# Hybrid diffusion step on one core: 28 adaLN pieces from TensorE matmuls to VectorE row sums

## The chip, the core and the metric

The kernel is one program on one NeuronCore of one Trainium2 chip. The metric is the device time of one execution in microseconds (us); lower is better. Three timed runs of the kernel before gave a median of 3042.03 us (3039.22 to 3045.7).

## What is computed

One inference step through two trunk layers (L = 2) for 128 context and 512 latent tokens, T = 640 in all, D = 1024. What matters here of a layer:

```
m = silu(c) @ w_mod[l] + b_mod[l]          # [6 * 1024], for c_ctx (context) and c (latent)
sh1, sc1, g1, sh2, sc2, g2 = split(m, 6)   # parts 0 to 5
h = rmsnorm(x) * (1 + sc1) + sh1
...                                        # four mixers on h, gated and merged
x = x + g1 * merged
h2 = rmsnorm(x) * (1 + sc2) + sh2
x = x + g2 * (square(relu(h2 @ w_fc1)) @ w_fc2)
```

The vector m (adaLN) depends on the conditioning alone, not on x, so it can be made at any time before its use. All data are float32.

## The kernel before

Activations lie transposed, channels on the 128 partitions and tokens along the row. Every large product is done in three matmuls on split operands (a high part and the rest, low): `mm3_step`, lines L225 to L227, 128 x 128 weights against 320 tokens. A *block* is one panel of 128 output channels: 8 k-tiles x 3 matmuls for each half (320 tokens) of T, 48 in all, into one of the two `dn` PSUM banks per half. The weights of a block come as two tiles `wr` on SyncE's DMA queue (L202); ScalarE casts the high part `wh` (L214), and VectorE, or in every third case GpSimd, subtracts the low part `wl` (`sub_lo`, L198). All three rings hold four tiles, two blocks.

The program runs a prologue, then for each layer the mixers (with an order of steps written out in `PLAN`), the output projection (8 blocks), a norm, and the MLP. The MLP goes in four quarters q: 8 blocks of fc1, each half emptied by `squares` (Relu on ScalarE, L1754; product r on VectorE, L1755; cast and `sub_lo` into `fh`, `fl`), then 8 blocks of fc2, each half emptied by `residual` on VectorE (L1547). The order in which instructions stand on each engine is made by a scheduler from the program's order and priorities, and each engine then runs its queue in that order.

adaLN is made in *pieces* of 256 outputs, four to a part, so 24 a layer. `adaln` does a piece on TensorE: 8 small matmuls of `cpad` (the two conditioning vectors, padded to 32 columns) against the weight rows (L290), a copy to SBUF on ScalarE (L295), two matmuls with `sel` that turn the row into columns (L297), and an add of the bias on VectorE (L300) into `mods[l]`. Layer 0's parts 0 and 1 are made in the prologue. The rest go through the generator `adaln_ahead`, which loads four [128, 512] tiles `wa` (256 KB each, ring of 8) per piece and makes one piece per step: 4 during the first mixers, 8 during layer 0's output projection, and then 28 (4 of layer 0's part 5, 24 of layer 1) in layer 0's MLP, where `between`, called after each block, takes five steps of the chain `bgen` in eight blocks. The same chain holds `s5_build` for layer 1 (9 steps): tables for the S5 mixer, complex products `cmul` with one real product on VectorE (L595), its twin on GpSimd (L596) and their sum on VectorE (L597), and small matmuls (L635, L662, L668).

Of the kernel before, what the change touches and what calls it, by code (L numbers as in the profile page):

```python
# [13 lines left out]
F32 = mybir.dt.float32  # L14
# [9 lines left out]
D = 1024  # L24
# [20 lines left out]
RINGS = dict(  # L45
    t1=3, tx=4, tq=6, ty=2, tw=5, td=5, nt=4, wa=8, wr=4, wh=4, wl=4, fh=10,
)
# [28 lines left out]
def hybrid_body(ctx: ExitStack, tc: tile.TileContext, a: dict, o: dict, dbg: dict):  # L76
# [79 lines left out]
    def wa(shape, name):  # L156
        return ring("wa", 512, "ada" if "ada" in top else "pool")(shape, name)

# [148 lines left out]
    def adaln_ahead(l, parts, after=()):  # L307

        for part in parts:
            for q in range(4):  # L310
                halves = {}

                def raw(part, n, q=q, halves=halves):
                    if n not in halves:
                        halves[n] = wa([128, 512], "wa")
                        sp.dma_start(
                            out=halves[n], in_=a["w_mod"][l, part * 4 + q, n // 2][:, (n % 2) * 512:(n % 2) * 512 + 512]
                        )
                    return halves[n]
# [156 lines left out]
    def s5_build(l, where, after):  # L476
# [116 lines left out]
        def cmul(out, xr, yr, xi, yi, op, shape):  # L593
            u, v = big(shape, "s5u", bufs=2, where=where), big(shape, "s5v", bufs=2, where=where)
            nc.vector.tensor_tensor(out=u, in0=xr, in1=yr, op=ALU.mult)  # L595
            nc.gpsimd.tensor_tensor(out=v, in0=xi, in1=yi, op=ALU.mult)  # L596
            nc.vector.tensor_tensor(out=out, in0=u, in1=v, op=op)  # L597
# [945 lines left out]
    def residual(l, part, ps, hf, f, x):  # L1543

        for s, c0, c1 in streams(hf):
            xs = x[:, f, hf * HF + c0:hf * HF + c1]
            nc.vector.scalar_tensor_tensor(  # L1547
                out=xs, in0=ps[:, c0:c1], scalar=mods[l][:, part * 8 + f, s:s + 1], in1=xs, op0=ALU.mult, op1=ALU.add
            )


# [17 lines left out]
    with tc.tile_pool(name="pro", bufs=1, reuse_waits="tile") as pool:  # L1569
# [11 lines left out]
        def panel_adaln(parts, q, acc, out):  # L1581
            w = {part: [big([128, 1024], "wm", bufs=WM) for _ in range(2)] for part in parts}
            for part in parts:
                for i in range(2):
                    sp.dma_start(out=w[part][i], in_=a["w_mod"][0, part * 4 + q, i])
            if soon:
# [37 lines left out]
        build_after[0] = h[1][0:1, KT - 1, T - 1:T].bitcast(F32)  # L1624
        adgen = adaln_ahead(0, range(2, 6), {4: 1})

    for l in range(L):
# [97 lines left out]
        with ExitStack() as mlp:  # L1725
# [3 lines left out]
            acc_n = big([128, T], "acc_n")  # L1729

            def res(part, squares, f, hf, ps):
                residual(l, part, ps, hf, f, x)
                if squares:
                    square_into(acc_n, x, f, hf)

            for f in range(KT - NTAIL):
# [15 lines left out]
            def squares(act, j, hf, ps):  # L1752
                r = t1([128, HF], "r2")
                nc.scalar.activation(out=r, in_=ps, func=AF.Relu)  # L1754
                nc.vector.tensor_tensor(out=r, in0=r, in1=ps, op=ALU.mult)  # L1755
                hi, lo = hsl(act[j], 0, hf)
                nc.scalar.copy(out=hi, in_=r)
                sub_lo(lo, r, hi)

            act0 = []  # L1760
# [24 lines left out]
            def between():  # L1785
                nonlocal turn
                turn += 1
                step(bgen, turn * 5 // 8 - (turn - 1) * 5 // 8)

            for q in range(4):  # L1790
# [4 lines left out]
                for f in range(KT - NTAIL if q == 3 and l + 1 < L else KT):  # L1795
# [42 lines left out]
def _pack(inp):  # L1838
# [3 lines left out]
    for n, s in sizes.items():  # L1842
# [11 lines left out]
    p["x_t"] = np.concatenate([inp["x_prompt"][0], inp["x_sample"][0]], 0).T.reshape(KT, 128, T).transpose(1, 0, 2)  # L1854
    p["c_t"] = np.stack([_col(inp["c_ctx"]), _col(inp["c"][0])], -1)
    p["w_mod"] = st([
        st([
            w.reshape(2, 4, 128, 24, 256)[s, :, :, q].transpose(1, 0, 2).reshape(128, 1024) for q in range(24) for s in range(2)
        ]).reshape(24, 2, 128, 1024) for w in inp["w_mod"]
    ])  # L1860
    p["b_mod"] = _col(inp["b_mod"])
# [126 lines left out]
```

## Time and profile before

| | us |
|---|---|
| median of 3 runs (lowest, highest) | 3042.03 (3039.22, 3045.7) |
| the profiled execution, its own time | 3031.18 |
| span of its profile, first to last instruction | 3029.4 |
| TensorE busy (share of the span) | 2841.5 (94%) |
| VectorE busy | 1724.3 (57%) |
| ScalarE busy | 1180.8 (39%) |
| GpSimd busy | 970.2 (32%) |

The profile is one execution, 10.9 us below the median of the timed runs. Matmuls are pipelined, so a busy TensorE is not one at its peak: how many matmuls it starts in a stretch says more. TensorE's granted clock is full (1.00) in the stretches that are spoken of below but for the one that ends at 1088 us.

### The profile page before, as it was taken

To read this page: it belongs to the slowest core of one execution; us is meant where nothing else is said; L and a number is where in the kernel's file an instruction comes from. 1 tells how busy PE (TensorE), PEld (TensorE's weight loads), DVE (VectorE), ACT (ScalarE), POOL (GpSimd) and SP (SyncE) were. 2 spreads that over 40 slices of the span, in tenths; PEclk is the share of its full clock that TensorE was granted. 3 is DMA by queue.
4 is the path that set the end of the run, shared out by engine and by line. 5 is a ranking of instruction groups with operands and counts; after the bars stand their busy time and mean duration, and the time that the engine had idled before them with its cause. 6 is when DMAs were issued, how large, how long until landed. Compare 5 with 4: busy or idle time off the path is not lost.

```text
span 3029.4 us, 54102 instructions
## 1 busy us (share of the span) xinstructions
PE 2841.5 (94%) x20782; PEld 2663.8 (88%) x20782; DVE 1724.3 (57%) x3730; ACT 1180.8 (39%) x2660; POOL 970.2 (32%) x1057
## 2 busy tenths in 40 slices
PE   7888898999899999999999889999999999999999
PEld 5888788898689888899998879888898999999999
DVE  7859847765643456646235686475666436433333
ACT  4343463343344242323234536523535434322322
POOL 3737506523212222424111670264131122211111
PEclk9989999999899999999999999999999999999999
DMA  6752253224432735434444323431252323222222
GB/s 238 239 180 90 71 152 111 81 90 134 145 109 72 239 102 174 146 115 154 153 146 132 121 82 111 140 107 58 91 181 86 110 87 112 63 77 74 74 77 84
DMA packets 241858, 364.21 MB, mean 120 GB/s; under 512 B 42272, under 2 KB 104480, under 8 KB 241600
## 3 DMA queue, kind: packets, MB, share of 16 engines
q1 hardware_dynamic: 226848, 336.97, 35.5%
q10 hardware_dynamic: 14752, 23.78, 2.1%
q8 instruction: 164, 2.69, 0.4%
q14 instruction: 94, 0.77, 0.1%
HBM read 294.98 MB, written 65.68 MB: 119 GB/s over the span
## 4 chain that ended last, share of the span: by engine, by line
PE 71%; DVE 15%; issue 4%; DMA 3%; ACT 3%; POOL 2%; SPq 0%; ACTq 0%; DVEq 0%; POOLq 0%
PE dn L225 20%; PE dn L226 19%; PE dn L227 19%; DVE wl L198 2%; DVE B L767 2%; PE mx L290 1%; PE mx L1287 1%; PE pb L1331 1%; PE mx L1461 1%; PE mx L1325 1%; PE mx L1416 1%; DMA sseg<-acum 1%; DVE sc L764 1%; DVE sc L765 1%; PE mx L745 1%
## 5 line engine op out<-in xcount | busy, mean ns | idle before, releaser
L198 POOL TENSOR_TENSOR wl<-wr,wh 128x512 fp32r<-128x512 f32 x207 | 282.6, 1366 | 1271.2 <-ACT wh L214 1151.3
L214 ACT CAST wh<-wr 128x512 fp32r<-128x512 f32 (+1 forms) x614 | 377.4, 620 | 612.9 <-PE dn L226 539.6
L198 DVE TENSOR_TENSOR wl<-wr,wh 128x512 fp32r<-128x512 f32 (+1 forms) x407 | 325.7, 804 | 304.7 <-ACT wh L214 297.3
L225 PE MATMUL dn<-hh,wh 128*128 128x320 f32 x1328 | 422.6, 319 | 8.4 <-ACT us L697 2.7
L227 PE MATMUL dn<-hh,wl 128*128 128x320 f32 x1328 | 420.2, 317 | 3.4 <-DVE wl L198 3.4
L226 PE MATMUL dn<-hl,wh 128*128 128x320 f32 x1328 | 420.1, 316 | 2.8 <-DVE hl L403 1.5
L225 PE MATMUL dn<-nh,wh 128*128 128x320 f32 x992 | 311.7, 315 | 6.6 <-DVE r L1755 6.6
L225 PE MATMUL dn<-fh,wh 128*128 128x320 f32 x1008 | 313.6, 311 | 2.0 <-DVE s5u L595 1.3
L226 PE MATMUL dn<-nl,wh 128*128 128x320 f32 x992 | 308.9, 312 | 3.9 <-DVE nl L403 1.6
L227 PE MATMUL dn<-fh,wl 128*128 128x320 f32 x1008 | 312.0, 310 | 0.0
L226 PE MATMUL dn<-fl,wh 128*128 128x320 f32 x1008 | 311.8, 309 | 0.0
L227 PE MATMUL dn<-nh,wl 128*128 128x320 f32 x992 | 308.0, 311 | 0.0
L226 PE MATMUL dn<-wl,hh 128*128 128x256 f32 (+1 forms) x880 | 258.2, 294 | 16.3 <-DVE wl L198 14.2
L225 PEld LDWEIGHTS dn<-hh,wh 128*128 128x128 f32 x1328 | 254.3, 192 | 16.5 <-issue 3.1
L225 PE MATMUL dn<-wh,hh 128*128 128x256 f32 (+1 forms) x880 | 259.7, 297 | 8.5 <-DVE dtraw L1216 4.2
L227 PEld LDWEIGHTS dn<-hh,wl 128*128 128x128 f32 x1328 | 254.2, 191 | 8.9 <-DVE wl L198 4.6
L226 PEld LDWEIGHTS dn<-hl,wh 128*128 128x128 f32 x1328 | 254.2, 191 | 7.1 <-POOL hl L198 2.1
L227 PE MATMUL dn<-wh,hl 128*128 128x256 f32 (+1 forms) x880 | 257.1, 293 | 0.0
L1547 DVE SCALAR_TENSOR_TENSOR x<-dn,mod,x 128x192 f32<-128x192 f32 (+2 forms) x240 | 98.0, 437 | 225.2 <-PE dn L227 222.2
L225 PE MATMUL dn<-B,wh 128*128 128x320 f32 x640 | 207.8, 326 | 15.1 <-ACT B L834 4.4
L226 PE MATMUL dn<-B,wh 128*128 128x320 f32 x640 | 203.4, 318 | 0.0
L227 PE MATMUL dn<-B,wl 128*128 128x320 f32 x640 | 201.3, 315 | 0.0
(400 smaller groups left out, 6715.0 us busy)
## 6 DMA issues: line engine op xcount, KB each, us to landing
wr<-in_w_fc_dram SPq DMA_DIRECT2D x256, 256.0 KB, 2.8
wa<-in_w_mod_dram SPq DMA_DIRECT2D x160, 256.0 KB, 4.5
wr<-in_w_gate_dram SPq DMA_DIRECT2D x128, 256.0 KB, 2.8
wr<-in_w_tok_dram SPq DMA_DIRECT2D x80, 256.0 KB, 2.9
wr<-in_w_branch_dram SPq DMA_DIRECT2D x64, 256.0 KB, 3.0
acc<-gth SPq DMA_DIRECT2D x48, 320.0 KB, 3.0
gold<-acc SPq DMA_DIRECT2D x48, 320.0 KB, 3.3
gate<-gah ACTq DMA_DIRECT2D x70, 160.0 KB, 2.0
```

Source lines behind the costliest of these rows:

```text
L198: engine.tensor_tensor(out=out, in0=full, in1=hi, op=ALU.subtract)
L214: nc.scalar.copy(out=hi, in_=raw)
L225: nc.tensor.matmul(ps, sh, vh, start=first, stop=False)
L226: nc.tensor.matmul(ps, sh, vl, start=False, stop=False)
L227: nc.tensor.matmul(ps, sl, vh, start=False, stop=last)
L290: nc.tensor.matmul(acc[r0:r0 + 32, i * 256:i * 256 + 256], cpad[:, k, :], raw(part, k // 2)[:, c0:c0 + 256], start=(n_ < 4), stop=(n_ >= 4),)
L745: nc.tensor.matmul(xs[:, ri, g * NI:(g + 1) * NI], pm[:, ri, g * 128:(g + 1) * 128], U[:, g0 + g], start=True, stop=True)
L764: ve.tensor_tensor(out=pair[:, 0], in0=src, in1=re.to_broadcast(shp), op=ALU.mult)
L765: ve.tensor_tensor(out=pair[:, 1], in0=src[:, :, ::-1], in1=im.to_broadcast(shp), op=ALU.mult)
L767: ve.tensor_tensor(out=dst, in0=dst, in1=pair[:, i], op=ALU.add)
L1287: nc.tensor.matmul(sc[:, n, c0:c0 + (k1 - k0) * 128], qT[rows[n], g, ct], kT[rows[n], k0:k1].rearrange("p k c -> p (k c)"), start=True, st ...
L1547: nc.vector.scalar_tensor_tensor(out=xs, in0=ps[:, c0:c1], scalar=mods[l][:, part * 8 + f, s:s + 1], in1=xs, op0=ALU.mult, op1=ALU.add)
```

## The change

Layer 0's parts 2 to 4 stay as they were, except that `wa` is now a ring of three [128, 1024] tiles (512 KB). The other 28 pieces become `adaln_rows`: w_mod transposed lies in DRAM, a tile of 128 outputs (rows) by 1024 inputs is loaded, and VectorE multiplies it with the conditioning vector and sums each row in one instruction (`tensor_tensor_reduce`), once for each of the two conditioning vectors, with the bias as the sum's start. The product itself goes to a PSUM tile that nobody reads. That is 56 tiles and 112 row sums. The conditioning vectors, silu applied, are written to DRAM in the prologue and broadcast to all partitions (`cb`, 1 MB) before each MLP. One row sum is taken after each half block, held by the scheduler behind the instruction that empties the half's bank (`fill`); 96 fall into layer 0's MLP and 16 into layer 1's. `between` now steps `s5_build` alone, once in six blocks, and the scratch tiles of its products have one buffer instead of two in the MLP.

```diff
 RINGS = dict(
-    t1=3, tx=4, tq=6, ty=2, tw=5, td=5, nt=4, wa=8, wr=4, wh=4, wl=4, fh=10,
+    t1=3, tx=4, tq=6, ty=2, tw=5, td=5, nt=4, wa=3, wr=4, wh=4, wl=4, fh=10,
 )
...
+    cr = tmp([128, 16], "cr", bufs=1)
+    sp.dma_start(out=cr, in_=a["c_rows"])
+    crt = tmp([128, 16], "crt", bufs=1)
+    nc.scalar.activation(out=crt, in_=cr, func=AF.Tanh, scale=0.5)
+    nc.vector.tensor_scalar(out=crt, in0=crt, scalar1=0.5, scalar2=0.5, op0=ALU.mult, op1=ALU.add)
+    nc.vector.tensor_tensor(out=cr, in0=cr, in1=crt, op=ALU.mult)
+    c_d = dp.tile([128, 16], F32, name="c_d")
+    sp.dma_start(out=c_d, in_=cr)
...
+    def cond_rows():
+
+        cb = big([128, 2, D], "cb")
+        sp.dma_start(out=cb.rearrange("p s k -> p (s k)"), in_=c_d.rearrange("a b -> (a b)").unsqueeze(0).to_broadcast((128, 2 * D)))
+        return cb
+
+    def adaln_rows(l, parts, cb, after=()):
+
+        for part in parts:
+            for f in range(part * 8, part * 8 + 8):
+                with tc.high_priority(offset=AHEAD):
+                    w = wa([128, D], "wa")
+                    sp.dma_start(out=w, in_=a["w_modt"][l * 48 + f - 40])
+                prod = mx().rearrange("p a b -> p (a b)")
+                for s in range(2):
+                    nc.vector.tensor_tensor_reduce(
+                        out=prod, in0=w, in1=cb()[:, s], scale=1.0, scalar=bmod[l][:, f:f + 1], op0=ALU.mult,
+                        op1=ALU.add, accum_out=mods[l][:, f, s:s + 1],
+                    )
+                    if s and f % 8 == 7 and part in after:
+                        make_gsc(l, after[part])
+                    yield
...
         def cmul(out, xr, yr, xi, yi, op, shape):
-            u, v = big(shape, "s5u", bufs=2, where=where), big(shape, "s5v", bufs=2, where=where)
+            u, v = (big(shape, t, bufs=2 if where == "build" else 1, where=where) for t in ("s5u", "s5v"))
...
+            def fill(ins):
+
+                with tc.issue_after(ins.ins):
+                    step(rows)
+
             def res(part, squares, f, hf, ps):
-                residual(l, part, ps, hf, f, x)
+                ins = residual(l, part, ps, hf, f, x)
                 if squares:
                     square_into(acc_n, x, f, hf)
+                fill(ins)
...
             def squares(act, j, hf, ps):
                 r = t1([128, HF], "r2")
                 nc.scalar.activation(out=r, in_=ps, func=AF.Relu)
-                nc.vector.tensor_tensor(out=r, in0=r, in1=ps, op=ALU.mult)
+                ins = nc.vector.tensor_tensor(out=r, in0=r, in1=ps, op=ALU.mult)
                 hi, lo = hsl(act[j], 0, hf)
                 nc.scalar.copy(out=hi, in_=r)
                 sub_lo(lo, r, hi)
+                fill(ins)
...
-            bgen = [adgen]
+            cb = cond_rows()
+            step(adgen, 99)
+            rows, bgen = adaln_rows(l, (5,), lambda: cb), iter(())
             if l + 1 < L:
-                bgen += [
-                    adaln_ahead(l + 1, (0, 1), {1: 0}),
-                    s5_build(l + 1, "mlp", lambda: act0[7][1][0:1, 0, T - 1:T].bitcast(F32)),
-                    adaln_ahead(l + 1, range(2, 6), {4: 1}),
-                ]
-            bgen = itertools.chain(*bgen)
+                rows = itertools.chain(rows, adaln_rows(l + 1, range(5), lambda: cb, {1: 0, 4: 1}))
+                bgen = s5_build(l + 1, "mlp", lambda: act0[7][1][0:1, 0, T - 1:T].bitcast(F32))
...
-                step(bgen, turn * 5 // 8 - (turn - 1) * 5 // 8)
+                step(bgen, int(turn % 6 == 0))
```

What this makes of the instructions' order is shown at three places, as they stand in each engine's queue. Rows of the changed kernel carry its own line numbers: L1795 there is L1755 before, L1578 is L1547, L626 and L628 are L595 and L597, L354 is the new row sum.

The first place is VectorE in the first quarter of layer 0's MLP, where fc1's halves are emptied. Before:

```order
L1755 TENSOR_TENSOR r_2382_12528<-r_2382_12528,dn_12503 128x320
L198 TENSOR_TENSOR fl_12092<-r_2382_12528,fh_12091 128x320
L198 TENSOR_TENSOR wl_12660<-wr_12657,wh_12659 128x512
L198 TENSOR_TENSOR wl_12666<-wr_12663,wh_12665 128x512
L1755 TENSOR_TENSOR r_2384_12558<-r_2384_12558,dn_12533 128x320
L198 TENSOR_TENSOR fl_12092<-r_2384_12558,fh_12091 128x320
L300 TENSOR_TENSOR mod_93<-mx_12571,bmod_89 128x4
L1755 TENSOR_TENSOR r_2398_12622<-r_2398_12622,dn_12597 128x320
L198 TENSOR_TENSOR fl_12094<-r_2398_12622,fh_12093 128x320
```

And in the changed kernel (an ISA row of 128x1024 is a row sum's pass, the one of 128x1 behind it the read-out of the sum):

```order
L1795 TENSOR_TENSOR r_2367_12529<-r_2367_12529,dn_12504 128x320
L354 ISA mx_12502,mod_101<-wa_12500,cb_12378,bmod_97 128x1024
L354 ISA mod_101 128x1
L198 TENSOR_TENSOR fl_12052<-r_2367_12529,fh_12051 128x320
L1795 TENSOR_TENSOR r_2375_12572<-r_2375_12572,dn_12547 128x320
L354 ISA mx_12579,mod_101<-wa_12577,cb_12378,bmod_97 128x1024
L354 ISA mod_101 128x1
L198 TENSOR_TENSOR fl_12054<-r_2375_12572,fh_12053 128x320
L198 TENSOR_TENSOR wl_12692<-wr_12689,wh_12691 128x512
```

The add of L300 is gone, and behind each product r that empties a bank stands a row sum; the subtractions of `fl` and `wl` come behind it.

The second place is VectorE near the end of the S5 build, which in the changed kernel lies between fc2's residuals; `s5qt` with `s5u` as its source is a product's last add. Before, it stood among fc1's products:

```order
L618 COPY s5bz_15832<-s5bt_15820 128x8x16
L595 TENSOR_TENSOR s5u_15870<-s5pou_14290,s5nc_15862 128x512
L597 TENSOR_TENSOR s5qt_15864<-s5u_15870,s5v_15871 128x512
L1755 TENSOR_TENSOR r_2993_15781<-r_2993_15781,dn_15756 128x320
```

In the changed kernel:

```order
L1578 SCALAR_TENSOR_TENSOR x_11260<-dn_15749,mod_101,x_11260 128x128
L1578 SCALAR_TENSOR_TENSOR x_11260<-dn_15749,mod_101,x_11260 128x192
L354 ISA mx_15778,mod_102<-wa_15776,cb_12378,bmod_98 128x1024
L354 ISA mod_102 128x1
L681 TENSOR_SCALAR s5nc_17198<-s5c_17154 128x128
L705 SCALAR_TENSOR_TENSOR s5ks_16721<-i_105,s5d_12973,s5ks_16721 128x16
L647 COPY s5bz_17168<-s5bt_17156 64x8x16
L648 COPY s5bz_17168<-s5bt_17156 64x8x16
L649 COPY s5bz_17168<-s5bt_17156 128x8x16
L626 TENSOR_TENSOR s5u_17206<-s5pou_12968,s5nc_17198 128x512
L198 TENSOR_TENSOR wl_15880<-wr_15877,wh_15879 128x512
L628 TENSOR_TENSOR s5qt_17200<-s5u_17206,s5v_17207 128x512
L1578 SCALAR_TENSOR_TENSOR x_11260<-dn_15780,mod_101,x_11260 128x320
L354 ISA mx_15778,mod_102<-wa_15776,cb_12378,bmod_98 128x1024
```

The row sum at the head of these rows is the 75th, and this add of `s5qt` is S5's last; S5's first operation on VectorE stands right behind the 11th row sum. The two rows of `s5u` and `s5qt` now have a subtraction of weights between them.

The third place is the head of SyncE's DMA queue. Before:

```order
L116 DMA cs<-in_c_t_dram 128x16
L1585 DMA wm_121<-in_w_mod_dram 128x1024
L1585 DMA wm_122<-in_w_mod_dram 128x1024
L1585 DMA wm_123<-in_w_mod_dram 128x1024
L1585 DMA wm_124<-in_w_mod_dram 128x1024
L113 DMA ident<-in_ident_dram 128x128
```

In the changed kernel:

```order
L116 DMA cs<-in_c_t_dram 128x16
L283 DMA cr_89<-in_c_rows_dram 128x16
L1617 DMA wm_129<-in_w_mod_dram 128x1024
L1617 DMA wm_130<-in_w_mod_dram 128x1024
L1617 DMA wm_131<-in_w_mod_dram 128x1024
L1617 DMA wm_132<-in_w_mod_dram 128x1024
L289 DMA c_d<-cr_89 128x16
L113 DMA ident<-in_ident_dram 128x128
```

The load of the conditioning rows goes second, and their store to DRAM, which waits for three operations on them, stands ahead of the identity and all that follows it.

## Rows read from the trace of the kernel before

**Rows 1.** The page: part 1 (busy time), part 4 (chain that ended last).

```profile
PE 2841.5 (94%) x20782; PEld 2663.8 (88%) x20782; DVE 1724.3 (57%) x3730; ACT 1180.8 (39%) x2660; POOL 970.2 (32%) x1057
...
PE 71%; DVE 15%; issue 4%; DMA 3%; ACT 3%; POOL 2%; SPq 0%; ACTq 0%; DVEq 0%; POOLq 0%
```

**Rows 2.** Stretches: busy PE, PEld, DVE, ACT, POOL; clock, DMA share, GB/s.

```profile
1000.00:1088.00 88.00, 85.28 (x622) 74.96 (x621) 42.44 (x115) 28.19 (x64) 12.08 (x11) 0.96 0.66 222
1088.00:1610.00 522.00, 510.93 (x3938) 475.44 (x3938) 264.28 (x542) 159.10 (x328) 144.93 (x131) 1.00 0.44 142
1360.00:1410.00 50.00, 47.07 (x437) 44.67 (x437) 42.95 (x69) 18.01 (x40) 28.44 (x26) 1.00 0.51 170
2600.00:2700.00 100.00, 100.00 (x684) 100.00 (x683) 32.51 (x64) 28.26 (x55) 16.29 (x14) 1.00 0.24 74
```

**Rows 3.** The same view, L225 alone: busy, (count), then its loads.

```profile
1088.00:1610.00 522.00, 309.06 (x980) 184.09 (x981) 1.00 0.44 142
```

**Rows 4.** The same for L290 (adaLN).

```profile
1088.00:1610.00 522.00, 33.12 (x432) 12.71 (x432) 1.00 0.44 142
```

**Rows 5.** TensorE in order of time around one piece; start, length, then what.

```profile
1157.01 0.31 PE L226 MATMUL dn<-fl,wh 128*128 128x320 f32 x1
1157.16 0.50 PE L297 MATMUL mx<-sel,mrow 128*128 128x2 f32 x4
...
1157.75 0.31 PE L225 MATMUL dn<-fh,wh 128*128 128x320 f32 x1
...
1160.40 0.31 PE L225 MATMUL dn<-fh,wh 128*128 128x320 f32 x1
1160.64 1.07 PE L290 MATMUL mx<-wa,cpad 128*32 128x256 f32 x16
...
1161.89 0.31 PE L227 MATMUL dn<-fh,wl 128*128 128x320 f32 x1
```

**Rows 6.** The view of rows 3 for the S5 lines L662, L635, L668.

```profile
1088.00:1610.00 522.00, 14.56 (x256) 7.94 (x256) 1.00 0.44 142
...
1088.00:1610.00 522.00, 11.61 (x64) 8.24 (x64) 1.00 0.44 142
...
1088.00:1610.00 522.00, 3.51 (x128) 2.79 (x128) 1.00 0.44 142
```

**Rows 7.** Single operations: min/median/max ns; groups (busy, mean ns); one in time.

```profile
L198 DVE TENSOR_TENSOR wl<-wr,wh x407: 629/693/1868, 27.3 to 3010.2; 128x512 fp32r<-128x512 f32 x135, 128x544 fp32r<-128x544 f32 x1
L198 DVE TENSOR_TENSOR fl<-r,fh x88: 474/492/1611, 1090.6 to 2971.1; 128x320 fp32r<-128x320 f32 x88
...
L198 DVE TENSOR_TENSOR wl<-wr,wh 128x512 fp32r<-128x512 f32 x403 | 322.3, 803 | 304.7 <-ACT wh L214 297.3 <-PE dn L227 5.7 <-PE mx L1325 0.4
...
L1120 ACT ACTIVATION_READ_ACCUMULATOR sot<-xs 128x1 f32 x10 | 1.9, 189 | 0.0
...
L595 DVE TENSOR_TENSOR s5u<-s5pin,s5bt 128x512 f32<-128x512 f32 x16 | 21.5, 1347 | 0.2
...
L391 DVE SCALAR_TENSOR_TENSOR nh<-x,gsc,mx 128x320 f32<-128x320 f32 x32 | 15.7, 540 | 1.3 <-PE mx L374 1.3
...
58.82 0.55 DVE L403 SCALAR_TENSOR_TENSOR hl<-nh,mod,hh 128x320 fp32r<-128x320 f32 x1 [0.17 <-ACT hh L402]
```

**Rows 8.** The view of rows 3 for VectorE's S5 product lines L595, L597.

```profile
1088.00:1610.00 522.00, 42.52 (x48) 1.00 0.44 142
...
1088.00:1610.00 522.00, 31.94 (x48) 1.00 0.44 142
```

**Rows 9.** The first microseconds in order of time (SPq is SyncE's queue).

```profile
0.73 0.40 SPq L116 DMA_DIRECT2D cs<-in_c_t_dram  x1
...
2.99 0.17 DVE L279 TENSOR_TENSOR cpad<-cs,csg 128x16 f32<-128x16 f32 x1
...
3.07 0.54 SPq L113 DMA_DIRECT2D ident<-in_ident_dram  x1
```

More of the change, by code (lines that the diff above doesn't have):

```diff
@@ L156, in wa @@
     def wa(shape, name):
-        return ring("wa", 512, "ada" if "ada" in top else "pool")(shape, name)
+        return ring("wa", 1024, "ada" if "ada" in top else "pool")(shape, name)
     def big(shape, tag, dt=F32, bufs=1, where="pool"):
@@ L313, in raw @@
                 def raw(part, n, q=q, halves=halves):
[L314 to L319, printed above, removed]
+                    if n // 2 not in halves:
+                        halves[n // 2] = wa([128, 1024], "wa")
+                        sp.dma_start(out=halves[n // 2], in_=a["w_mod"][part * 4 + q, n // 2])
+                    return halves[n // 2][:, (n % 2) * 512:(n % 2) * 512 + 512]
                 for n in range(KT // 2):
@@ L1546, in residual @@
             xs = x[:, f, hf * HF + c0:hf * HF + c1]
-            nc.vector.scalar_tensor_tensor(
+            ins = nc.vector.scalar_tensor_tensor(
                 out=xs, in0=ps[:, c0:c1], scalar=mods[l][:, part * 8 + f, s:s + 1], in1=xs, op0=ALU.mult, op1=ALU.add
             )
+        return ins
     def h_tiles(name):
@@ L1584, in panel_adaln @@
                 for i in range(2):
-                    sp.dma_start(out=w[part][i], in_=a["w_mod"][0, part * 4 + q, i])
+                    sp.dma_start(out=w[part][i], in_=a["w_mod"][part * 4 + q, i])
             if soon:
@@ L1624, in hybrid_body @@
         build_after[0] = h[1][0:1, KT - 1, T - 1:T].bitcast(F32)
-        adgen = adaln_ahead(0, range(2, 6), {4: 1})
+        adgen = adaln_ahead(0, (2, 3, 4), {4: 1})
     for l in range(L):
@@ L1729, in hybrid_body @@
             acc_n = big([128, T], "acc_n")
+            rows = iter(())
+            def fill(ins):
+                with tc.issue_after(ins.ins):
+                    step(rows)
             def res(part, squares, f, hf, ps):
-                residual(l, part, ps, hf, f, x)
+                ins = residual(l, part, ps, hf, f, x)
                 if squares:
                     square_into(acc_n, x, f, hf)
+                fill(ins)
             for f in range(KT - NTAIL):
@@ L1802, in hybrid_body @@
             step(bgen, 99)
+            step(rows, 99)
             if l + 1 < L:
@@ L1855, in _pack @@
     p["c_t"] = np.stack([_col(inp["c_ctx"]), _col(inp["c"][0])], -1)
+    p["c_rows"] = np.stack([inp["c_ctx"], inp["c"][0]]).reshape(128, 16)
+    w = inp["w_mod"][0].reshape(2, 4, 128, 24, 256)
     p["w_mod"] = st([
[L1857 to L1860, printed above, removed]
+        w[s, :, :, q].transpose(1, 0, 2).reshape(128, 1024) for q in range(20) for s in range(2)
+    ]).reshape(20, 2, 128, 1024)
+    p["w_modt"] = np.concatenate([inp["w_mod"][0].T.reshape(48, 128, D)[40:], inp["w_mod"][1].T.reshape(48, 128, D)])
     p["b_mod"] = _col(inp["b_mod"])
```

## The prediction

> **What bounds the kernel now.** I read the page first, then stretches of the program, then single lines. The page has TensorE busy 94% of the span and holding 71% of the chain that ended last; VectorE has 15% of that chain, DMA 3% [rows 1]. So work taken off TensorE is worth its own length, as long as what replaces it is not late.
>
> The stretch that matters is the MLP of layer 0, 1088 to 1610 us: all but one of the 28 pieces in question run there. The busy times by stretch [rows 2] show TensorE at 511 of its 522 us and VectorE at 264; the MLP of layer 1 shows TensorE's pace with nothing in its way, 684 matmuls in 100 us or 146.2 ns each, a block of 48 in 7.02 us, with VectorE busy 32.5 of 100. Line by line, the layer-0 stretch holds 980 matmuls of each of L225, L226 and L227 [rows 3]; 2940 at 146.2 ns are 430 us. The other 92 us are three things:
>
> - adaLN: 432 records of L290 [rows 4], 16 to a piece, so 27 pieces. What a piece costs is read from the order in time [rows 5]: two dense matmuls that start 1.49 us apart around the 16 records (1160.40 to 1161.89) would start 0.29 apart without them, which is 1.20; the four records of L297 stretch 0.29 to 0.74 (1157.01 to 1157.75), 0.45. Together 1.65 us, and 27 of them 44.5 us.
> - the S5 build: at most the 14.6 + 11.6 + 3.5 = 30 us of its three lines [rows 6].
> - what is left, 92 - 44.5 - 30 = 18 us: TensorE waiting.
>
> **The change, part by part.**
>
> *TensorE's pieces go.* 28 x 1.65 = **46.2 us off**; the 28th stands in the norm just before the stretch. That is path. The ScalarE copies and small VectorE adds of a piece go too, worth nothing: nobody but the piece waits for them.
>
> *Row sums come:* 112, each a pass over 1024 columns and a read-out of the sum, 96 in the layer-0 MLP and 16 in layer 1. No row shows VectorE summing while it multiplies, so neighbours give the price [rows 7]. The subtraction of two SBUF tiles takes 693 ns (median) at 512 columns and 492 at 320: 1.047 ns a column, so 1.23 us at 1024. ScalarE's read-out of a sum is 189 ns. The subtraction's mean is 803, 0.11 above its median, because it now and then meets GpSimd. I take 1.23 + 0.11 + 0.19 = 1.53 us. The low end is the bare slope with a hidden read-out, 1.07. The high end is what S5's product on VectorE suffers beside its twin on GpSimd: 1347 ns for the 512 columns that cost 693 undisturbed, a factor of 1.94, so 1.23 x 1.94 + 0.19 = 2.58. The subtraction decides because it is nearest: two f32 SBUF inputs, and spread over the same blocks.
>
> Behind a row sum queue, on VectorE, the low part of the next weights (TensorE waits for it, but its ring is two blocks deep, 14 us) and the low part of the activation (needed in the second product). The bank is already empty; the next half's evacuation meets at most the end of a row sum, 1.5 us, against the 3.5 us that the other bank lasts. One row sum alone therefore stops nothing. Their sum can.
>
> *S5 steps one block in six.* The program asks for them over 49 blocks, but in the order shown VectorE has S5's first operation behind the 11th row sum and its last product behind the 75th, so 64 row sums, 32 blocks. That is where VectorE is fullest. It has there: 32 blocks at 2.28 us, the rate of layer 1's MLP (32.5 us for 684 / 48 = 14.25 blocks [rows 2]), 73 us; 64 x 1.53 = 98 us; and S5 itself, between 74 us (its product lines, 42.5 + 31.9 [rows 8]) and 125 (264 less 61 blocks at 2.28), of which I take 100. Together 271 us, against 32 x 7.02 + 30 = 255 on TensorE: 16 us of waiting that nothing hides. On top, a full VectorE holds TensorE up at single places; from 1360 to 1410, with VectorE at 43 of 50 us, TensorE is busy 47.1 [rows 2], so it lost 2.9 us of 50: 271 / 50 x 2.9 = 16. So 32 us of waiting in place of 18, **14 given back**. The scratch tiles of a product go from two buffers to one, so GpSimd can't run ahead; that is inside these 16, and I charge nothing more.
>
> *Layer 1's MLP* takes 16 x 1.53 = 24 us of VectorE beside an engine idle for 67 of 100 us: nothing. If that cover failed it would cost those 24 at most.
>
> *SyncE's queue at the start.* The copy of the conditioning rows to DRAM waits for a load, a Tanh and two VectorE operations, with everything from the identity on queued behind it. The present chain of that kind runs from the issue at 0.73 to 3.16 us; the identity was issued at 3.07 [rows 9]. The new chain begins 0.45 later and ends near 3.7, its issue takes 0.4: the queue is late by about 1.1 us. I charge 1 (0 to 2).
>
> *The output projection, 1000 to 1088 us.* It takes 8 pieces through three slots of 512 KB where eight of 256 KB were, and the 1 MB broadcast of the conditioning rows lands in the same stretch, the fullest of these for DMA: 66%, 222 GB/s [rows 2]; 1 MB at that rate is 4.7 us of transfer. A weight load queued behind a slot that isn't free would stop TensorE. Between 0 and 10 us; I charge 2, since the pieces that were loaded ahead for the MLP leave the stretch.
>
> *Everything else* keeps its work, but the scheduler's order shifts in small ways on every engine: 0, give or take 6.
>
> Sum: 46.2 - 14 - 1 - 2 = **29 us less**. The profiled execution took 3031.2, so 3002; the median of the runs, 3042.0, is 10.9 above that execution, and I carry this over: **3013 us**.
>
> **A rule that speaks against it.** The rows first: a VectorE operation with a scalar and two f32 SBUF inputs takes 0.55 us at 320 columns, and 0.54 with one input in PSUM [rows 7], so two SBUF inputs alone cost no second cycle. Neither carries a sum along. The Trainium skill, "Vector Engine (DVE) Microarchitecture Reference", section "Points that are easy to get wrong", says that the scalar-tensor-tensor shape with two SBUF sources that are not bf16 runs at half throughput, since both read ports are taken and none is left for the accumulator. By that rule a column would take two cycles and the time would be the first rival's; no row here shows VectorE with its accumulator.
>
> **The rivals.**
>
> *A row sum takes two passes' time (slower).* By the slope: 1.23 + 1.07 + 0.19 = 2.49 us. The 32 S5 blocks then need 73 + 159 + 100 = 332 us of VectorE against 255, 77 us of waiting; the 16 blocks with row sums alone 116 against 112. With the 16 that is 97 in place of 18: 46 - 79 - 3, 36 us slower, 3078. It decides from the price at which waiting reaches 18 + 43 us, 16 of them not VectorE's sum: 64 row sums in 255 + 45 - 173 = 127 us, 2.0 us each. For it: no row has the operation, and its two inputs meet GpSimd as S5's do. Against it: the pair of rows above. Chance 0.15.
>
> *VectorE keeps up (faster still).* If successive operations overlap enough that 255 us suffice, and thinner S5 halves the 18 us to 9: 46.2 + 9 - 3 = 52 us less, 2990. For it: the layer-0 waits sit where S5 is dense. Against it: the 271. Chance 0.15.
>
> *SyncE blocks (no change).* The load of a row tile waits for the row sum three tiles back, and the dense weights are queued behind it. If VectorE falls back by more than the 14 us of the weights' ring, each of the 48 tiles can hold TensorE; at 0.6 us each the 29 are gone: 3042. For it: the order of issue is fixed and a lag adds up. Against it: a tile serves a whole block, and three are in flight. Chance 0.12.
>
> **How the numbers follow.** The forecast has 0.58; its own range, with 1.07 to 1.9 us a row sum and the small terms at their ends, is 2988 to 3035. A measurement of this kernel can tell about 0.2%, 6 us, from no change. Faster: 0.55 of the forecast, the second rival, 0.03 of the third, 0.73. Same: 0.09. Slower: the first rival and the rest of the third, 0.18. The range leaves out the slow rival and a little below: 2986 to 3047.
>
> **What would show it.** Right: no L290 after 1100 us; passes near 1.3 us, read-outs under 0.2; the layer-0 MLP some 32 us shorter, VectorE over 90% busy in its S5 part and TensorE waiting there for VectorE; layer 1's MLP still at 146 ns a matmul. Wrong: row sums of 2 us and more; TensorE waiting for weights whose DMA is late; a loss before 1088 us.

## The result

The changed kernel takes 3009.24 us (median of 4 runs, 3006.22 to 3011.15), beside 3040.62 for the kernel before: a ratio of 0.9893, with 95% between 0.9876 and 0.9910, so 31.4 us less. The prediction was 3013. The profiled execution of after took 3008.78, right on its median; the one of before lay 9.4 under its median of 3040.62. With 1.8 us outside the span, as before, its span is 3007.0. So the two traces differ by only 22.4 us where the medians differ by 31.4, and below, traces are compared stage by stage and never by their totals.

The page of after, parts 1 and 4:

```profile
PE 2810.5 (93%) x20222; PEld 2650.8 (88%) x20222; DVE 1868.3 (62%) x3928; ACT 1169.7 (39%) x2633; POOL 972.3 (32%) x1057
...
PE 33%; DVE 3%; DMA 1%; POOL 1%; issue 1%; ACT 1%; SPq 0%; DVEq 0%; POOLq 0%; ACTq 0%
```

TensorE is 31 us less busy than in [rows 1], VectorE 144 us more. The chain is followed over 40% of the span only, so its shares don't compare with those of before. The stretches of [rows 2], with the S5 part of the layer-0 MLP (1159 to 1424) and the first 100 us of layer 1's MLP:

```profile
1000.00:1088.00 88.00, 83.08 (x613) 75.83 (x612) 41.55 (x116) 28.53 (x66) 14.22 (x13) 0.94 0.61 219
1088.00:1610.00 522.00, 495.30 (x3537) 476.07 (x3535) 407.21 (x768) 161.11 (x330) 160.78 (x135) 0.98 0.43 141
2580.00:2680.00 100.00, 100.00 (x684) 100.00 (x683) 51.11 (x94) 28.07 (x53) 18.37 (x14) 1.00 0.32 101
...
1159.00:1424.00 265.00, 243.94 (x1855) 234.12 (x1854) 253.84 (x449) 71.42 (x146) 110.99 (x93) 0.97 0.52 167
```

In the S5 part VectorE (third number) is busy 254 of 265 us and TensorE idle for 21, at a granted clock of 0.97 where all of the stretch had 1.00 before. In layer 1 TensorE keeps its 684 matmuls in 100 us, though VectorE now works 51 of them. The row sum, by line:

```profile
L354 DVE CUSTOM_DVE_ANT_0 mx<-wa,cb,bmod x112: 1274/1285/2259, 1110.7 to 2630.8; 128x1024 f32<-128x1024 f32 x112
L354 DVE DVE_READ_ACCUMULATOR2_ANT mod<- x112: 131/140/145, 1112.0 to 2632.0; 128x1 f32 x112
```

Whom TensorE waits for between the first product r of the layer-0 MLP and layer 1's S5 (us, times, longest), after:

```profile
PE dn L225 <- DVE r L1795: 13.0, 9, 2.8
PE dn L225 <- DVE x L1578: 4.4, 4, 1.3
PE pb L666 <- DVE s5pt L628: 3.8, 4, 1.7
```

and before:

```profile
PE dn L225 <- DVE r L1755: 7.2, 7, 1.4
PE mx L374 <- DVE ry L188: 1.8, 2, 1.2
PE mx L290 <- DMA wa<-in_w_mod_dram: 1.6, 2, 0.9
```

**One account for all kernels.** The stage from the layer-0 MLP's first r to layer 1's first S5 matmul holds nearly all that differs. There I took the time from each matmul's start to the next one's and held it against the undisturbed price of its kind: 146.3 ns dense, 89 for an S5 transpose, 25 and 15 for S5's narrow matmuls (as they stand in e3, 32 and 16 in a row), 62 and 110 for adaLN's, near their means in e5. A dense matmul is one of L225 to L227, with 128 columns of weights; a narrow one has 32. What is over is put down to a *wait* where TensorE sat idle over 0.15 us until VectorE was ready; else to the *clock* where it was granted at half; else to *mixing* where an S5 matmul stands next to it. The undisturbed prices add up to 525 us with the pieces on TensorE and to 485 to 487 without them. What neither they nor a column has is 10 to 13 us without the pieces and 16 to 22 with them (adaLN's own mixing, waits for others, the norm's small matmuls, scatter). All in us; the median is of all runs, the stage and the three columns are of one trace each, which may lie off its median (before 9.4 under, e2 8 over, e3 7 under).

| kernel | median | stage | waits for VectorE | half clock | mixing |
|---|---|---|---|---|---|
| before | 3040.6 | 575.4 | 16.2 | 1.5 | 11.0 |
| after | 3009.2 | 549.5 | 30.2 | 8.6 | 12.8 |
| e1 no row sums | 2983.6 | 526.6 | 14.7 | 5.0 | 9.6 |
| e2 two buffers | 3018.2 | 563.4 | 31.1 | 15.0 | 17.9 |
| e3 S5 held | 2995.2 | 529.2 | 26.6 | 4.1 | 1.0 |
| e4 S5's old places | 3009.0 | 547.3 | 35.5 | 13.7 | 1.1 |
| e5 pieces, S5 spread | 3035.2 | 574.0 | 10.7 | 11.4 | 10.1 |
| e6 held, 3 gaps | 2984.2 | 521.5 | 21.6 | 3.1 | 0.5 |
| e7 half rows | 3013.3 | 555.4 | 22.0 | 10.7 | 24.2 |
| e8 held, two buffers | 3002.2 | 537.0 | 32.2 | 7.1 | 1.1 |
| e9 held, half rows | 2990.8 | 524.0 | 22.0 | 4.2 | 0.5 |
| e10 held, no rows | 2979.7 | 517.2 | 16.2 | 3.8 | 0.8 |
| e11 pieces, S5 held | 3036.1 | 574.4 | 27.1 | 4.4 | 2.5 |
| e12 held, 2 gaps | 2993.8 | 524.7 | 23.5 | 4.2 | 0.5 |

Before the stage, traces with the very same start differ by as much as 8 us before the first residual (1001.1 us in e6, 1009.4 in e9), which is why the stage is the better measure.

### The profile page after: what moved, and what is told of

The parts are those of the page before. It is cut to its first block, busy times and chain, and to the rows that moved or that the text cites. A ratio compares the mean times of both kernels' runs of the same rounds, so it can differ in the third digit from the quotient of the medians.

```text
span 3007.0 us, 52966 instructions
## 1 busy us (share of the span) xinstructions
PE 2810.5 (93%) x20222; PEld 2650.8 (88%) x20222; DVE 1868.3 (62%) x3928; ACT 1169.7 (39%) x2633; POOL 972.3 (32%) x1057
## 5 line engine op out<-in xcount | busy, mean ns | idle before, releaser
L198 POOL TENSOR_TENSOR wl<-wr,wh 128x512 fp32r<-128x512 f32 x207 | 289.4, 1398 | 1212.6 <-ACT wh L214 1141.4
L225 PE MATMUL dn<-hh,wh 128*128 128x320 f32 x1328 | 426.0, 321 | 7.8 <-ACT gah L1520 3.2
L226 PE MATMUL dn<-hl,wh 128*128 128x320 f32 x1328 | 422.6, 318 | 3.1 <-DVE hl L434 1.8
L227 PE MATMUL dn<-hh,wl 128*128 128x320 f32 x1328 | 421.1, 318 | 2.3 <-DVE wl L198 2.3
L225 PE MATMUL dn<-nh,wh 128*128 128x320 f32 x992 | 311.6, 315 | 11.3 <-DVE r L1795 10.3
L225 PE MATMUL dn<-fh,wh 128*128 128x320 f32 x1008 | 314.5, 312 | 5.6 <-DVE x L1578 3.4
L226 PE MATMUL dn<-nl,wh 128*128 128x320 f32 x992 | 310.8, 314 | 4.2 <-DVE nl L434 1.9
L226 PE MATMUL dn<-fl,wh 128*128 128x320 f32 x1008 | 312.6, 310 | 0.1
L227 PE MATMUL dn<-fh,wl 128*128 128x320 f32 x1008 | 312.5, 310 | 0.0
L227 PE MATMUL dn<-nh,wl 128*128 128x320 f32 x992 | 309.7, 312 | 0.0
L226 PE MATMUL dn<-wl,hh 128*128 128x256 f32 (+1 forms) x880 | 259.1, 295 | 15.0 <-DVE wl L198 12.9
L225 PEld LDWEIGHTS dn<-hh,wh 128*128 128x128 f32 x1328 | 256.4, 193 | 17.4 <-issue 4.0
L225 PE MATMUL dn<-wh,hh 128*128 128x256 f32 (+1 forms) x880 | 259.4, 297 | 5.2 <-ACT wh L214 2.4
L226 PEld LDWEIGHTS dn<-hl,wh 128*128 128x128 f32 x1328 | 256.1, 193 | 8.5 <-issue 2.6
L227 PEld LDWEIGHTS dn<-hh,wl 128*128 128x128 f32 x1328 | 255.7, 193 | 6.8 <-DVE wl L198 3.5
L227 PE MATMUL dn<-wh,hl 128*128 128x256 f32 (+1 forms) x880 | 257.6, 294 | 0.0
L225 PE MATMUL dn<-B,wh 128*128 128x320 f32 x640 | 206.9, 324 | 17.7 <-ACT B L865 6.3
L1578 DVE SCALAR_TENSOR_TENSOR x<-dn,mod,x 128x192 f32<-128x192 f32 (+2 forms) x240 | 97.7, 436 | 176.1 <-PE dn L227 170.7
L226 PE MATMUL dn<-B,wh 128*128 128x320 f32 x640 | 203.3, 318 | 0.2 <-DVE B L198 0.2
L225 PEld LDWEIGHTS dn<-nh,wh 128*128 128x128 f32 x992 | 188.8, 191 | 15.5 <-DVE r L1795 12.6
```

Of the source, the lines that this page charges most:

```text
L198: engine.tensor_tensor(out=out, in0=full, in1=hi, op=ALU.subtract)
L225: nc.tensor.matmul(ps, sh, vh, start=first, stop=False)
L226: nc.tensor.matmul(ps, sh, vl, start=False, stop=False)
L227: nc.tensor.matmul(ps, sl, vh, start=False, stop=last)
L1578: ins = nc.vector.scalar_tensor_tensor(out=xs, in0=ps[:, c0:c1], scalar=mods[l][:, part * 8 + f, s:s + 1], in1=xs, op0=ALU.mult, op1=ALU.add)
```

## The experiments

Each ratio is taken against runs of the kernel before beside it (medians 3037.8 to 3039.1), with its 95% interval in brackets.

**e1: the whole cost of the row sums.** No row sums, row tiles or copy of the conditioning rows; their results are constants:

```diff
+    nc.gpsimd.memset(mods[0][:, 40:48], 0.0)
+    nc.gpsimd.memset(mods[1], 0.0)
...
-            cb = cond_rows()
...
-            rows, bgen = adaln_rows(l, (5,), lambda: cb), iter(())
+            rows, bgen = iter(()), iter(())
...
-                rows = itertools.chain(rows, adaln_rows(l + 1, range(5), lambda: cb, {1: 0, 4: 1}))
```

> This kernel leaves out the 112 row sums, their tile loads and the broadcast of the conditioning rows, so layer 0's part 5 and all of layer 1's adaLN are constants; TensorE's 28 pieces stay out as in the change. Theory (VectorE is overfull where row sums and S5 meet, 1159 to 1333 us, and gives back some 15 us of the 46): with the row sums gone TensorE's waiting in the layer-0 MLP falls to 18 us or less, and the time is 2985 to 2995, 14 to 24 us under the changed kernel's 3009. Rival (the row sums are hidden, and what is given back comes from the single scratch buffer of S5's products): 3006 to 3011, as the changed kernel.

2983.6 us, ratio 0.9826 [0.9806, 0.9846], where the theory had it or a little under. The row sums cost 25.6 us together by medians, 20 by ratios, either within some 8 by the intervals. In the traces it is 23 in the stage: 15.5 as waits for VectorE, 3.6 as half clock, 3.2 as mixing.

**e2: GpSimd may run ahead.** Two buffers for its S5 product, one for the small S5 load:

```diff
-            u, v = (big(shape, t, bufs=2 if where == "build" else 1, where=where) for t in ("s5u", "s5v"))
+            u, v = (big(shape, t, bufs=2 if where == "build" or t == "s5v" else 1, where=where) for t in ("s5u", "s5v"))
...
-            braw = big([128, 2, 4, 16], "s5b", bufs=2, where=where)
+            braw = big([128, 2, 4, 16], "s5b", bufs=1, where=where)
```

> The changed kernel with two buffers again for the scratch tile that GpSimd writes in S5's products (and one instead of two for the small S5 input b, to make room). Theory (VectorE's sum of work): within 4 us of the changed kernel, 3005 to 3013, VectorE as full between 1159 and 1333 us as before. Rival (GpSimd can't run ahead, VectorE's adds wait for it): 8 us or more under the changed kernel, 3001 or less, with GpSimd's waits on VectorE's adds (50 us in that stretch) mostly gone.

3018.2 us, 0.9934 [0.9916, 0.9953]: 9 us slower than after, which neither theory had. The account shows no more waiting for VectorE, but more half clock and mixing. The single load buffer also touched the prologue, so e8 repeats it cleanly.

**e3: S5 steps held**, like the row sums, behind the evacuation of the block's last bank:

```diff
+            emptied = [None]
...
+                emptied[0] = ins
...
-                step(bgen, int(turn % 6 == 0))
+                if turn % 6 == 0:
+                    with tc.issue_after(emptied[0].ins):
+                        step(bgen)
```

> The changed kernel with the VectorE instructions of each S5 step held behind the last bank evacuation of the block after which the step is taken, so that S5 is spread over all 96 row sums and beyond instead of ending behind the 75th. Theory (VectorE's sum of work in the S5 part): VectorE needs some 390 us over the 460 of the whole MLP, so spread evenly it is under 90% everywhere, and half or more of the given-back time returns: 2995 to 3003, 6 to 14 us under the changed kernel. Rival (a row sum at a bad place stops TensorE singly, however full VectorE is): within 4 us of the changed kernel, 3005 to 3013.

2995.2 us, 0.9852 [0.9830, 0.9873]: 14 us under the changed kernel, as the theory had it. But the account says where: 12 of the stage's 20 us are mixing, 4.5 the clock, and only 4 waits. The theory named VectorE's load; by these two traces most of the gain is TensorE's order. S5's 256 narrow matmuls of L693 come in eight groups of 32. In the changed kernel five groups stand in a row, two are split in four, and the last stands two at a time between dense matmuls (TensorE in order of time; start, length):

```profile
1474.51 0.38 PE L693 MATMUL pb<-s5qt,s5bz 128*32 128x112 f32 x2
1474.82 0.41 PE L226 MATMUL dn<-fl,wh 128*128 128x320 f32 x1
1475.16 0.38 PE L693 MATMUL pb<-s5qt,s5bz 128*32 128x112 f32 x2
1475.46 0.41 PE L227 MATMUL dn<-fh,wl 128*128 128x320 f32 x1
1475.81 0.38 PE L693 MATMUL pb<-s5qt,s5bz 128*32 128x112 f32 x2
```

One dense matmul and two narrow ones come every 0.65 us, so a pair costs 0.65 - 0.15 = 0.50 us. In e3 all eight groups stand in a row:

```profile
1219.80 0.97 PE L693 MATMUL pb<-s5qt,s5bz 128*32 128x112 f32 x32
1220.59 0.23 PE L699 MATMUL pb<-s5c,s5bz 128*32 128x16 f32 x8
1220.65 0.23 PE L699 MATMUL pb<-s5nc,s5bz 128*32 128x16 f32 x8
1220.82 0.41 PE L227 MATMUL dn<-nh,wl 128*128 128x320 f32 x1
```

The 32 start within 0.79 us, 0.05 a pair. The kernel before has such alternations too, in two of its eight groups, so the change itself adds little mixing (12.8 for 11.0).

**e4: S5 steps at their old places in the program:**

```diff
-                step(bgen, int(turn % 6 == 0))
+                step(bgen, turn * 5 // 8 - (turn - 1) * 5 // 8 if turn > 20 else 0)
```

> The changed kernel with the S5 steps at the places in the program where they were before the change (9 steps behind blocks 21 to 34, five in eight) instead of one in six blocks. The scheduler takes S5's instructions as early as they are ready, and its VectorE order ends S5 behind the 68th row sum here, the 75th in the changed kernel. Theory: the steps' places in the program hardly matter, 3005 to 3014. Rival (one in six blocks is what keeps VectorE from filling up): 3017 or more, 8 us above the changed kernel.

3009.0 us, 0.9899 [0.9881, 0.9917], as the theory had it. By the account that is two differences which cancel: hardly any mixing here (1.1 for 12.8), but more waits (35.5) and half clock (13.7).

**e5: the kernel before, S5 steps one in six.** The pieces stay on TensorE:

```diff
-                    s5_build(l + 1, "mlp", lambda: act0[7][1][0:1, 0, T - 1:T].bitcast(F32)),
...
+                sgen = s5_build(l + 1, "mlp", lambda: act0[7][1][0:1, 0, T - 1:T].bitcast(F32))
...
+                step(sgen, int(turn % 6 == 0))
```

> The kernel before, with its pieces on TensorE, and S5 steps one block in six as in the change. Theory: the pace in the program changes little, since the scheduler takes S5 as soon as it is ready; 3039, give or take 6, so that the pieces taken off TensorE alone are worth 3039 - 2984 = 55 us, 9 more than the 46 of the prediction. Rival: the pace itself gains what the surplus of 9 is, so 3030 (3026 to 3033), and the pieces are worth their 46.

3035.2 us, 0.9989 [0.9972, 1.0006]: within the theory's 3039 give or take 6; its interval, 3030 to 3040, still touches the rival's range. The pace alone changes nothing that can be told. From e5 to e1 the pieces are worth 51.6 us by medians (within some 8), between the two theories.

**e7: half the length of every row sum** (512 of 1024 columns), all loads whole:

```diff
+    HALF = D // 2
...
-                        out=prod, in0=w, in1=cb()[:, s], scale=1.0, ...
+                        out=prod[:, :HALF], in0=w[:, :HALF], in1=cb()[:, s, :HALF], scale=1.0, ...
```

> The changed kernel with every row sum over the first 512 of its 1024 columns; all loads stay whole. It leaves out half of each adaLN sum. Theory (VectorE's time is the cost): each row sum is 0.62 us shorter, 40 us less VectorE in the S5 part, which had 171 busy of 174 us; most of the 26 us that row sums cost goes: 2991 (2985 to 2997). Rival (the cost is the 14 MB of loads and their place on SyncE's queue, or the order): 3005 to 3012.

3013.3 us, 0.9924 [0.9908, 0.9941]. The theory fell: 60 us of VectorE's work gone and not a microsecond won. The pass did get shorter, 752 ns for 1285, and the waits for VectorE did fall, from 30.2 us to 22.0, half way to the 14.7 of e1. Mixing, 11.4 us more, and half clock, 2.1 more, took that back. Two stretches of e7:

```profile
1190.00:1270.00 80.00, 66.25 (x547) 63.14 (x548) 77.51 (x133) 23.49 (x50) 44.59 (x40) 0.96 0.55 180
1290.00:1470.00 180.00, 180.00 (x1260) 170.19 (x1259) 115.85 (x246) 45.75 (x87) 50.52 (x44) 0.99 0.50 164
```

the same stretches of the changed kernel:

```profile
1190.00:1270.00 80.00, 69.79 (x566) 66.79 (x566) 79.29 (x125) 24.23 (x53) 42.24 (x35) 0.96 0.54 175
1290.00:1470.00 180.00, 172.13 (x1292) 165.98 (x1291) 155.04 (x262) 45.31 (x88) 63.39 (x52) 0.99 0.54 173
```

and L225 alone in them, e7 first (L226 and L227 have as many):

```profile
1190.00:1270.00 80.00, 40.61 (x122) 23.99 (x122) 0.96 0.55 180
1290.00:1470.00 180.00, 115.04 (x362) 68.33 (x361) 0.99 0.50 164
...
1190.00:1270.00 80.00, 43.14 (x133) 26.14 (x133) 0.96 0.54 175
1290.00:1470.00 180.00, 112.95 (x355) 67.13 (x355) 0.99 0.54 173
```

At its front S5 closes up into the time that the sums leave: from 1190 to 1270 VectorE is nearly as full as before, and TensorE starts fewer dense matmuls (122 of L225 for 133). Later VectorE is free (116 of 180) and TensorE never idle, yet it starts hardly more of them (362 for 355; the totals of 1260 and 1292 differ by S5's own): mixing, 24.2 us in the stage. But S5 as a whole doesn't shrink into free time. From its first product to its last add it takes, in the changed kernel, in e7 and in e1:

```profile
1191.50:1425.30 233.80, 212.76 (x1644) 203.20 (x1643) 223.19 (x364) 65.86 (x138) 105.88 (x90) 0.97 0.53 169
...
1182.10:1440.30 258.20, 244.01 (x1791) 228.52 (x1790) 200.04 (x386) 71.01 (x143) 102.42 (x92) 0.97 0.50 163
...
1165.50:1415.90 250.40, 242.84 (x1838) 230.86 (x1837) 161.20 (x273) 72.43 (x145) 100.39 (x93) 0.99 0.34 109
```

That is 234, 258 and 250 us, with VectorE busy for 95%, 77% and 64% of it. Why the scheduler puts more narrow matmuls between dense ones in e7 is open; that halving gains nothing holds for this one order. The rival's number is near. The loads it names are not the cause: e6 has all of them (28 MB in 56 tiles of 512 KB, not the 14 that the expectations of e6 and e7 have) and is 29 us faster than e7. The order, which it also names, is.

**e6: held, and gaps.** As e3, but no row sum behind the three evacuations that follow an S5 step, since 96 row sums have more evacuations than they need:

```diff
-            emptied = [None]
+            emptied, skip = [None], [0]
...
                 emptied[0] = ins
+                if skip[0]:
+                    skip[0] -= 1
+                    return
...
                         step(bgen)
+                    skip[0] = 3
```

> The version with held S5 steps, and in addition no row sum behind the three evacuations after each S5 step, so that the row sums fill the layer-0 MLP to its end. Theory (the cost that is left is VectorE being full in single blocks): 61 blocks at 2.28, 96 row sums at 1.43 and 100 of S5 are 376 us of VectorE against 458 of TensorE, evenly spread 82%; 4 to 8 us under the held version, 2989 (2984 to 2993). Rival (what is left is the 14 MB of row tiles and the copy, whatever VectorE does): the held version's time, 2995, give or take 4.

2984.2 us, 0.9825 [0.9800, 0.9851]. The interval lies clear of the changed kernel's; with the same row sums, this is the time that e1 has without any. Two stretches of S5, e6:

```profile
1190.00:1230.00 40.00, 39.65 (x313) 39.16 (x312) 32.30 (x56) 14.01 (x29) 17.98 (x15) 1.00 0.51 161
1240.00:1280.00 40.00, 38.23 (x302) 37.61 (x301) 31.96 (x51) 11.20 (x23) 14.27 (x12) 1.00 0.46 149
```

and after:

```profile
1190.00:1230.00 40.00, 35.63 (x270) 34.34 (x270) 39.60 (x68) 11.45 (x24) 19.36 (x16) 0.96 0.54 175
1240.00:1280.00 40.00, 34.99 (x305) 33.28 (x304) 39.63 (x65) 12.41 (x28) 19.08 (x18) 0.96 0.56 178
```

VectorE goes from 99% to 80% busy there, TensorE from 88% to 97%, and the clock back to 1.00.

**e8: held, with two buffers** for GpSimd's product in the MLP and the prologue left alone (e2's first edit on e3, and `bufs=2 if where == "build" else 1` for `s5b`).

> The version with held S5 steps, and in addition two buffers for GpSimd's product tile of S5 in the MLP (paid for with one buffer of the small S5 load there; the prologue keeps its two). Theory: the single buffer costs nothing, and the 9 us that two buffers lost without the hold came from the prologue's single load buffer and from S5 bunching: 2995, give or take 4. Rival (GpSimd that runs ahead meets VectorE's two-input passes more often and slows both): 3000 to 3005. A gain of over 5 us would say that the single buffer did cost.

3002.2 us, 0.9881 [0.9863, 0.9900]: the rival's number, 7 us over e3 by medians, though the intervals overlap. TensorE waits for r 16.4 us in e8 and 9.6 in e3 by the view of waits. But the rival's cause isn't borne out: VectorE's passes aren't longer (mean 1.40 us in e8, 1.43 in e3), nor are its S5 products (0.85 and 0.91). Whether a freer GpSimd makes r late, and why, is open.

**e9: held, half rows** (e7's edit on e3).

> The version with held S5 steps, and every row sum over the first 512 of its 1024 columns, all loads whole; it leaves out half of each adaLN sum. Without the hold, half rows gained nothing (3013), since S5 closed up: its narrow matmuls then stood between dense ones for 24 us more than in a row, in place of 12. With the hold they can't. Theory (then the length of a row sum does count, through the waits for VectorE, 26 us in the held version and 15 without row sums): 2986 (2981 to 2991). Rival (a row sum's length never counts, only where it stands): 2995, give or take 4.

2990.8 us, 0.9840 [0.9823, 0.9857]: 4 us under e3, inside the intervals, so the medians tell nothing between the two theories. The account, with one trace each, speaks for the first: without row sums (e10) the held order waits 16.2 us, with whole ones 26.6, with half ones 22.0. The free order has 14.7, 30.2 and 22.0 (e1, the changed kernel, e7). In either order the waits grow with a row sum's length, about in proportion.

**e10: held, no row sums** (e3's edit on e1).

> No row sums, no row tiles and S5 steps held. It leaves out the adaLN pieces in question. Theory: the hold takes away the 10 us in which S5's narrow matmuls stand between dense ones, and some of the low clock behind them: 2973 (2967 to 2978). Then the version with gaps (2984) still pays 11 for its row sums. Rival (the hold gains only by sparing a full VectorE): 2984, give or take 4, and the version with gaps has its row sums for nothing.

2979.7 us, 0.9798 [0.9782, 0.9814], between the theory and its rival. Mixing goes from 9.6 to 0.8, but the median by 4 only, and intervals overlap: whether the hold gains anything here is unclear. Against this floor e6 pays 4.5 us for its 112 row sums, in the stage 4.3; the intervals overlap, so it may be less.

**e11: pieces on TensorE, S5 held** (e3's edit on e5).

> The kernel before, pieces on TensorE, with S5 steps one block in six and held behind the block's last evacuation. Theory: S5's narrow matmuls stand in a row again, which gives back the 11 us that the trace of the unheld one shows, and a part of its 11 us at low clock: 3021 (3015 to 3027). Rival (with VectorE half idle the hold has nothing to order, and the pieces' own 62 and 110 ns matmuls keep the rest): 3035, give or take 4.

3036.1 us, 0.9993 [0.9984, 1.0002]: the rival's number. Mixing falls by 7.6 and half clock by 7.0, but waits rise from 10.7 to 27.1 (for r 10.3 by the view of waits, 2.2 in e5). Holding is no gain by itself; it paid (14 us, e3) where row sums fill VectorE.

**e12: two gaps for three.**

> The version with gaps, with two evacuations after each S5 step left without a row sum in place of three, so that the last row sums come 8 evacuations (four blocks, 28 us) earlier. Theory (with three gaps the row sums run into the norm behind the MLP, where TensorE waits 3 us for the squares' sum and shows 14.6 busy of 20): that wait falls to the 0.8 us it has elsewhere, the rest stays; 2982 (2977 to 2988), at or under the version with three gaps. Rival (the third gap is what spares S5's blocks): between that version and the held one without gaps, 2990 (2988 to 2995).

2993.8 us, 0.9846 [0.9817, 0.9874]: the rival's side by the median; the stage, 524.7 us, is nearer e6's. The wait for the squares' sum at the end did fall from 3.1 to 0.8, but waits for r rose from 5.8 to 10.6. The intervals of e3, e6 and e12 overlap, so among these the order is not settled; that each beats the changed kernel is.

## Why the prediction was right, and where it was not

*TensorE's pieces, 46.2 us.* Right: the base price of the stage falls by 39 us, with 4.9 of adaLN's mixing and 2.0 of waits for its tiles, 45.8 in the trace beside the 44.5 forecast there. By medians (e5 to e1) it is 51.6, within some 8; e5 also has 6.4 us more of half clock.

*A row sum, 1.53 us.* 1.285 + 0.140 = 1.43 by medians. In the layer-0 MLP the pass has a mean of 1.47 and a row sum takes 1.61; the 0.11 for meeting GpSimd was 0.19. From 512 to 1024 columns the pass grows by 533 ns, 1.041 a column, where the slope of two other subtractions [rows 7] gave 1.047.

The Trainium skill, "Vector Engine (DVE) Microarchitecture Reference", section "Points that are easy to get wrong", has the scalar-tensor-tensor shape with two SBUF sources that are not bf16 at half its throughput. The pass has two f32 SBUF sources and carries a sum, and shows no such halving: 1.041 ns a column. The trace lists it as a custom instruction (`CUSTOM_DVE_ANT_0`), so whether it is of that shape no run shows. By that rule the time would have been the first rival's 3078.

*The S5 part, 14 us given back.* The size is right: 30.2 us of waiting in the stage and 16.2 before, 14.0 apart. (In the MLP alone the views of waits add up to 22.3 and 9.4. So the levels, 32 and 18, were both too high: the 18 was what the other terms left over, and not all of it was waiting.) VectorE was busy 254 of 265 us there, near the sum of 271. The step that failed is the reason, "together 271 us, against 255 on TensorE: 16 us of waiting that nothing hides". It takes the 255 for a limit under which VectorE's sum costs nothing. With half row sums the 271 would be 237 and these 16 would be gone; e7's waits fall by 8 only, to 22.0, half way between the changed kernel's 30.2 and e1's 14.7. By the traces it is what stands ahead of one r that stops TensorE: in the changed kernel 12 of its 13 waits for an r or a residual have S5 operations among the five that VectorE did just before, and so have 6 of 7 in e1, where VectorE is busy for 64% of S5's stretch. The sum also says nothing of the order: e6 takes no operation off VectorE and is 25 us faster. Of its stage's 28 us, 12 are mixing, 9 waits and 5.5 half clock.

*What the sum lacked.* Half clock, 8.6 us after and 1.5 before, was not charged; in this trace each of its five stretches stands right behind waits. Mixing, 1.8 us more, wasn't either. For the stage the forecast had 44.5 - 14 = 30.5 us less. The traces have 45.8 - 14.0 - 7.1 - 1.8 and 3 us that no column has: 25.9 less. The medians moved by 31.4, 5.5 more than the stage, and starts before it vary by 8. So it is in part luck that the total came out 2 us from the forecast's 29, and the MLP got 25 us shorter (513.4 for 538.4, first r to last residual), not 32.

*SyncE's queue, 1 us; the output projection, 2 us.* The queue is as late as forecast: the identity is issued at 4.15 us, at 3.07 before. No cost of it can be seen: TensorE's first matmul starts at 4.95 us, at 5.07 before, and later starts vary by 8. The second was no loss: from the first residual to the first r it took 83.4 us for 85.5 (83.9 to 86.6 in the experiments with the same code there), with VectorE and DMA no busier than in [rows 2].

*Layer 1's MLP, nothing.* Right: from its first r to the end 451.1 us, and 451.5 before, with 16 row sums more on VectorE.

*The rivals.* Two passes' time: refuted by 1.43 us. VectorE keeps up: not in this kernel, with 30 us of waits; e6 reaches that rival's 2990 with another order. SyncE blocks: in the stage TensorE waits for no load after, and 2.0 us for the pieces' tiles before.

## What to carry to other kernels

A sum of the second engine's work, held against the first engine's time, can give the right size for a wrong reason. Before you price work that moves by its sum, ask what stands ahead of each operation that the first engine waits for, and what else is free to move: a scheduler may close up into the gap that a shorter operation leaves, and what the waits give back can go into a worse order on the first engine. Fix the place of both streams, spread them so that they don't meet, and then look at TensorE's order: narrow matmuls in one run, never two by two between wide ones.

## What the runs showed of the chip

Narrow matmuls put two by two between wide ones cost 0.50 us a pair (the changed kernel, 1474 to 1476 us), where a run of them costs 0.05 (e3, 1219.8 us), with TensorE shown as busy throughout.

The clock fell a little after the longest waits. TensorE in the changed kernel, around the longest wait for r:

```profile
1210.84 0.31 PE L227 MATMUL dn<-nh,wl 128*128 128x320 f32 x1
1213.92 0.42 PE L225 MATMUL dn<-nh,wh 128*128 128x320 f32 x1 [2.77 <-DVE r L1795]
1214.17 0.31 PE L226 MATMUL dn<-nl,wh 128*128 128x320 f32 x1
1214.32 0.31 PE L227 MATMUL dn<-nh,wl 128*128 128x320 f32 x1
...
1215.20 0.45 PE L227 MATMUL dn<-nh,wl 128*128 128x320 f32 x1
1215.44 0.47 PE L225 MATMUL dn<-nh,wh 128*128 128x320 f32 x1
1215.71 0.47 PE L226 MATMUL dn<-nl,wh 128*128 128x320 f32 x1
```

It comes back from 2.77 us of idleness at full pace (0.15 from start to start), and 1.3 us later the starts are 0.26 apart: 1.2 GHz for 2.4. The stretch of 1200 to 1220 us has a granted clock of 0.91. In e7 the clock also fell behind stretches of mixing in which TensorE is shown as busy, at 1491.5 us and at 1344.7:

```profile
1330.00:1344.70 14.70, 14.70 (x80) 8.42 (x78) 6.42 (x12) 1.24 (x2) 3.49 (x3) 1.00 0.34 120
1344.70:1348.10 3.40, 3.40 (x13) 3.08 (x14) 2.59 (x7) 0.36 (x1) 1.01 (x2) 0.50 0.00 0
```

So the waits alone don't tell the half clock: e5 has 10.7 us of waits and 11.4 of half clock, e11 27.1 and 4.4.
